# First half's moving operands made in four spaced steps, mean squares later, input rows added ahead of attention, the last pair's combining and loads sooner

## The chip, the cores and the metric

One NeuronCore of one Trainium2 chip. The metric is the device time of one execution in microseconds (us), the median of several runs. PE is TensorE (the matrix engine), DVE VectorE, ACT ScalarE, POOL GpSimd; SP, ACT and POOL also issue DMAs, each in the order of its own queue.

## What is computed

One decoder layer in float32, 2048 tokens by 1024: dilated causal attention (16 heads of 64, dilations 1, 4, 16, mixed by their softmax sums) beside a Mamba-2 scan (16 heads of 64, 2 groups, state 128), each gated and normalised, then one output product and a layer norm.

```python
proj = x @ w_in
q, k, v, z_att, z_ssm, xbc, dt = split(proj)
o1, o2, o3 (with l1, l2, l3) = windowed attention of q, k, v at dilations 1, 4, 16
y_att = rms_norm(softmax_mix(o1, o2, o3) * silu(z_att), att_norm_g)
xs, b, c = split(silu(causal_conv(xbc)))
y_ssm = rms_norm((ssd_scan(xs, dt, a, b, c) + d_skip * xs) * silu(z_ssm), ssm_norm_g)
out = concat(y_att, y_ssm) @ w_out
result = layer_norm(alpha * x + out, ln_g, ln_b)        # alpha = 2 ** 0.25
```

## The kernel before

Every float32 factor is kept as a high part, rounded to the type that PE multiplies quickly, and a low part, the remainder; a product is high x high + high x low + low x high, three matmuls. Making an operand is therefore a copy to `t[:, 0]` on ACT (high) and a subtraction to `t[:, 1]` on DVE (low), then a store to scratch memory in DRAM (names beginning with `d_`).

**0 to 207 us:** the V projection.

**207 to about 1490 us:** 52 jobs, each a 1024-deep product of two column tiles, done with Strassen and Winograd's seven products in place of eight. A product is 12 matmuls of 128 x 128 x 512 into one of five banks `pp` (lines L357, L359, L361). ACT empties a bank with `keep` (L366, tile `ev`), DVE adds (L374). The moving operands have the names B11, T1, B21, T2, B22, T4, T3; T... are differences of quarters. Jobs run in phases: ten on the first half of the tokens, 22 on the second, 12 more, and 8 output jobs (`"o"`) that multiply the scan's branch with W_out and leave their part of the output in `d_o`. After each product `flush()` runs the closures in `later[count]`, the count of products; `after(n, f)` puts `f` n products ahead. This written order is what PE, DVE, ACT and POOL execute; the order on SP's queue is set by a scheduler.

In the first phase four further things are made between the products: the second half's moving operands from x (`sums_part`, tiles `st` to `to`, stored to `d_T`), W_out's moving operands from rows times a gain (`output_side`, tiles `woraw` to `wot`, stored to `d_U`), the scan's gate (`fin_zs`, tile `ez`, to `d_zs`), and the decays of dt (`decays`, on DVE).

The scan has 32 units (16 blocks x 2 groups), one begun every four products from product 161 (about 740 to 1290 us). A unit goes through `ssd1` to `ssd7` in steps of a product; its matmuls use three banks `ss`. `ssd6` squares the gated rows and reduces them (L646, tile `bsh`), `ssd7` sums the result over the partitions with a matmul by ones (L651). `zt` is the gate's load.

**1490 to 2010 us:** attention, eight pairs of heads, 24 steps each, numbered (d, qd, half): `scores` (PE, L896; mask and minimum on DVE, L904; exponential on ACT, L912), `transposes` (L925, L927) and `values` (L945). `load_dil` brings a mask table `tb` and `v`. When a pair is through, `statistics` and `gather` send its sums through DRAM, `weights` makes the mixing weights on DVE, stored and loaded back broadcast as `wb`, and `combine` mixes the three results, for pairs 0 to 6 on POOL in four calls during the next pair (L1016, L1025, L1031), and stores columns of the attention branch, as raw rows in `d_ua` and, for row tiles 0 to 2, split in `d_uh`. Pair 7 is combined on DVE at the end.

**2010 us to the end:** sixteen row tiles of 128 tokens times W_out's attention half (`load_w`, eight tiles of 1 MB). For tiles 0 to 3 `product_early` does seven columns of eight, from `fetch_early`, and `product_last` the one of pair 7 (`e7`); for 4 to 15 `product` does all. Each tile is fetched raw (`fetch_raw`), split (`split`: L1081 high on ACT, L1082 low on DVE), squared (`squares`: L1087, L1088), and after its product `add` scales and adds it to `O[n]`, loaded from `d_o` by `residual_load` (L1093) after `residual_add` (L1099) added the input row there (L1096). `norm` is the layer norm: statistics (L1182, L1184), square root on ACT (L1186), normalising on DVE (L1196), gain and bias on POOL (L1197, L1198), and the store (L1199). `O[n]` of tile n uses the buffer of tile n - 4.

## Time and profile before

| what | value |
|---|---|
| runs | 2268.11, 2277.9 and 2277.93 us, median 2277.9 |
| profiled execution | 2259.55 us, its span 2257.7 us |
| mean granted clock of PE | 0.955 |
| DMA | 551.78 MB, mean 244 GB/s |

The span is the time from the profile's first to its last instruction; the execution's own time is a little longer. "Busy" is the share in which an engine executes. A row of waits reads: engine, what it was about to do and its line, `<-` what it waited for, then total us, times, and the longest. A row of a timeline reads: start, length, engine, line, operation, output `<-` inputs, with the idle time ahead in brackets. The granted clock is 1.00 or 0.50 in each moment.

### The profile page before, as it was taken

How to read it: one execution, taken by the hardware profiler on the slowest of the kernel's cores; microseconds unless marked ns; L12 is line 12 of the kernel's file. 1: busy time of each engine (PE TensorE's matmuls, PEld its weight loads, DVE VectorE, ACT ScalarE, POOL GpSimd, SP SyncE). 2: the span in 40 equal slices, each digit the busy share in tenths (PEclk: the TensorE clock that was granted, in tenths of full speed). 3: DMA queues.
4: the chain of work that ended last, by engine and by line, in shares of the span. 5: the costliest groups of instructions: out<-in, count | busy, mean ns of one | idle time of the engine just before them, and what ended most of it. 6: DMA issues, size and time to landing. Idle time of an engine off the chain costs nothing.

```text
span 2257.7 us, 39253 instructions
## 1 busy us (share of the span) xinstructions
PE 2066.3 (92%) x13768; PEld 1708.4 (76%) x13768; DVE 1438.5 (64%) x3235; ACT 1204.7 (53%) x3128; POOL 1188.7 (53%) x978
## 2 busy tenths in 40 slices
PE   7999896869999999988999989989999999988698
PEld 7998775648887777867777768878878887766576
DVE  3432654538999668755555433338888888856777
ACT  3331444425655676755656534447888888842121
POOL 2113444556887566664445344432566666770544
PEclk9999998989999999999999999979999999999899
DMA  9989675795777877799787893253687777796443
GB/s 334 370 316 332 232 272 204 246 389 162 226 219 267 313 262 274 261 344 342 230 271 248 293 366 111 100 181 131 197 244 215 199 218 227 214 338 190 157 170 111
DMA packets 273046, 551.78 MB, mean 244 GB/s; under 512 B 44689, under 2 KB 129553, under 8 KB 256081
## 3 DMA queue, kind: packets, MB, share of 16 engines
q1 hardware_dynamic: 185696, 261.09, 35.8%
q0 software_dynamic: 36448, 193.34, 24.0%
q10 hardware_dynamic: 50704, 94.84, 13.4%
q8 instruction: 109, 1.79, 0.3%
q14 instruction: 89, 0.72, 0.1%
HBM read 359.39 MB, written 206.57 MB: 251 GB/s over the span
## 4 chain that ended last, share of the span: by engine, by line
PE 34%; DMA 10%; DVE 9%; ACT 8%; issue 4%; POOL 2%; ACTq 1%; SPq 0%; DVEq 0%; POOLq 0%
PE S L896 5%; PE N L945 5%; PE T L925 5%; PE pp L357 5%; PE pp L359 5%; PE pp L361 5%; DMA zt<-d_zs 3%; ACT P L912 2%; ACT mt L578 1%; DVE P L904 1%; DMA TB22l<-d_UT 1%; DMA d_kl<-ev 1%; PE ss L618 1%; DMA kl<-d_kl 1%; DMA w<-d_wc 1%
## 5 line engine op out<-in xcount | busy, mean ns | idle before, releaser
L313 POOL TENSOR_TENSOR w<-wr,w 128x512 fp32r<-128x512 f32 x287 | 437.5, 1540 | 284.6 <-ACT w L312 212.4
L912 ACT ACTIVATE P<-P,st 128x256 f32<-128x256 f32 (+1 forms) x768 | 345.1, 451 | 99.4 <-DVE st L904 98.7
L904 DVE CUSTOM_DVE_ANT_0 P<-S,tb 128x256 f32<-128x256 f32 (+1 forms) x768 | 235.1, 362 | 87.0 <-PE S L896 49.6
L366 ACT COPY ev<-pp 128x512 f32<-128x512 f32 x208 | 121.1, 582 | 288.4 <-PE pp L361 188.7
L374 DVE TENSOR_TENSOR ev<-pp,ev 128x512 f32<-128x512 f32 x184 | 122.1, 684 | 167.4 <-PE pp L361 101.1
L927 DVE COPY PT<-T 128x512 f32<-128x512 f32 (+1 forms) x304 | 196.5, 677 | 1.4 <-PE T L925 1.4
L305 DVE TENSOR_TENSOR wr<-wr 128x512 f32<-128x512 f32 x164 | 173.2, 1056 | 35.7 <-DMA wr<-w 24.7
L312 ACT CAST w<-wr 128x512 fp32r<-128x512 f32 x287 | 171.2, 618 | 38.4 <-DVE wr L305 23.2
L925 PE MATMUL T<-ident,P 128*128 128x128 f32 x1200 | 179.3, 287 | 5.9 <-DVE PT L927 5.5
L945 PE MATMUL N<-PT,v 128*64 128x128 f32 x2400 | 176.8, 284 | 0.0
L945 PEld LDWEIGHTS N<-PT,v 128*64 128x64 f32 x2400 | 129.5, 138 | 33.3 <-issue 22.8
L925 PEld LDWEIGHTS T<-ident,P 128*128 128x128 f32 x1200 | 130.1, 143 | 30.3 <-DVE PT L927 7.2
L1016 POOL TENSOR_TENSOR wb<-num,wb 128x2048 f32<-128x2048 f32 x21 | 96.3, 4587 | 97.0 <-DMA wb<-d_wd 81.3
L912 ACT ACTIVATION_READ_ACCUMULATOR P<-P,st 128x1 f32 x768 | 143.8, 187 | 0.0
L896 PE MATMUL S<-kh,qp 64*128 64x256 f32 (+1 forms) x1024 | 126.5, 306 | 0.0
L414 DVE SCALAR_TENSOR_TENSOR ev<-ev 128x512 f32<-128x512 f32 x64 | 69.1, 1093 | 65.1 <-ACT ev L413 65.1
L463 DVE SCALAR_TENSOR_TENSOR acc<-U,cw,acc 128x2048 f32<-128x2048 f32 x36 | 106.5, 2959 | 3.4 <-ACT acc L460 3.0
L896 PEld LDWEIGHTS S<-kh,qp 64*128 64x128 f32 x1024 | 88.9, 188 | 22.1 <-issue 20.4
L148 PE MATMUL pp<-vh,xh 128*128 128x256 f32 (+1 forms) x320 | 91.4, 292 | 15.1 <-ACT xh L171 15.1
L357 PE MATMUL pp<-TT3h,w 128*128 128x512 f32 x176 | 77.1, 438 | 29.8 <-ACT ev L366 29.6
L141 POOL TENSOR_TENSOR vl<-vraw,vh 128x256 fp32r<-128x256 f32 (+1 forms) x32 | 29.9, 938 | 131.4 <-ACT vh L140 130.1
L357 PE MATMUL pp<-TB22h,w 128*128 128x512 f32 x208 | 87.1, 419 | 10.5 <-ACT ev L366 6.1
(476 smaller groups left out, 6084.5 us busy)
## 6 DMA issues: line engine op xcount, KB each, us to landing
wr<-w ACTq DMA_DIRECT2D x157, 256.0 KB
v<-d_v POOLq DMA_DIRECT2D x24, 1024.0 KB, 7.1
d_wc<-w SPq DMA_DIRECT2D x44, 512.0 KB
w<-d_wc POOLq DMA_DIRECT2D x44, 512.0 KB, 6.5
wb<-d_wd SPq DMA_DIRECT2D x42, 512.0 KB
csb<-d_cs ACTq DMA_DIRECT2D x32, 512.0 KB
st<-xT SPq DMA_DIRECT2D x31, 512.0 KB
d_v<-vt SPq DMA_DIRECT2D x16, 512.0 KB
```

The lines of the kernel that those rows point to most:

```text
L305: tt = lambda o, a, b, op=OP.subtract: nc.vector.tensor_tensor(q[o], q[a], q[b], op=op)
L312: nc.scalar.copy(t[:, 0], q[nm])
L313: nc.gpsimd.tensor_tensor(t[:, 1], q[nm], t[:, 0].bitcast(F32), op=OP.subtract)
L357: nc.tensor.matmul(ps, w[:, 0, k], th[:, k], start=start and k == 0, stop=False, skip_group_check=not start)
L366: nc.scalar.copy(e, ps)
L374: nc.vector.tensor_tensor(e, a, e, op=op)
L896: nc.tensor.matmul(ov(sp[h][:, 256 * b:256 * b + w]), A["q"][d][x][hr, blk], kv(A["k"][y][hr]), start=(m == 0), stop=(m == 2))
L904: nc.vector.tensor_tensor_reduce(P[:, h, b, 256 - w:256], sp[h][:, c0:c0 + w], tab[:, h, tab.shape[2] - w:], 1.0, 3.0e38, OP.add, OP.min, ...
L912: nc.scalar.activation(p, p, AF.Exp, bias=stat(A, 0, d, h, blk), scale=-1.0, accum_out=stat(A, 1, d, h, blk))
L925: nc.tensor.transpose(tp[:, h, b], P[:, h, b, 128 * which:128 * which + 128], ident)
L927: nc.vector.tensor_copy(pt[:, :, bl[0]:2], tp[:, :, bl[0]:2])
L945: nc.tensor.matmul(nm[64 * h:64 * h + 64, bq * 128:bq * 128 + 128], v[:, k, 64 * h:64 * h + 64], pts[which][:, h, b], start=(f or not whic ...
```

## The change

*Spaced steps.* `in_steps` puts one item of the first half in four successive products: subtraction, high, low, store. `token_sums` and `output_side` use it; loads come earlier, W_out's rows on SP's queue in eight buffers rather than ACT's in four, and the separate gain pass is gone (the gain is a factor in the copy and in the remainder). `ez` is one tile per column tile, stored on its own.

*Mean squares.* The reduction is `ssd7`, one product later, and the matmul `ssd8`, two later; `zt` is loaded one earlier.

*Input rows.* `fin_o` adds alpha times the input on DVE before `d_o` is stored; `residual_add` and its loads are gone at the end. The output jobs' first two operands lie in the buffers of attention's keys and queries.

*Attention.* Pair 0's tables are loaded on POOL's queue, its keys and queries within the last job. During pair 7 the weights and combining of pair 6 come earlier, loads of W_out partly too, and `fetch_early` takes all seven columns at once. At the end pair 7's `wb` loads stand ahead of rows, which move to ACT's and POOL's queues; squares are spread; norms 0 to 3 come after product 4; normalising is on ACT.

```diff
+        def in_steps(c, dst, k, name, o, bufs, queue, make=None, gain=None):
...
+            if make:
+                put(c, make)
+            put(c + 1, high)
+            put(c + 2, low)
+            put(c + 3, store)
+        def token_sums(k, b):
...
+                R[nm] = sums.tile([128, 512], F32, name="st", bufs=5)
...
+            for n, x in ((-7, ("11", 0, 0)), (-5, ("12", 0, 1)), (-4, ("22", 1, 1)), (-3, ("21", 1, 0))):
+                put(max(b + n, 0), lambda x=x: load(*x))
...
+                in_steps(b + c, d_T[1, nm], k, "to", lambda o=o: R[o], 3, nc.sync,
+                         lambda o=o, a=a, d=d: nc.vector.tensor_tensor(R[o], R[a], R[d], op=OP.subtract))
-                    R[nm] = sums.tile([128, 512], F32, name="woraw", bufs=4)
-                    nc.scalar.dma_start(R[nm], wout[e * 128:e * 128 + 128, c * 512:c * 512 + 512])
+                    R[nm] = sums.tile([128, 512], F32, name="woraw", bufs=8)
+                    nc.sync.dma_start(R[nm], wout[e * 128:e * 128 + 128, c * 512:c * 512 + 512])
-            def gain():
...
+                in_steps(at(c), d_U[nm], k, "wot", lambda o=o: R[o], 4, nc.gpsimd, make, gain)
-                output_side(k, 35 + 8 * k)
+                token_sums(k, 7 + 7 * k)
+                at = lambda c, k=k: 37 + (7 * k + c) * 30 // 28
+                output_side(k, at, 35 if k < 2 else 37 + (7 * k - 1) * 30 // 28 - 4)
-                if (ci, q) == (1, 0):
-                                          [[512, 128], [128 * 512, 16], [1, 128]]),
+                if q != ci:
+                                          [[512, 128], [128 * 512, 16], [1, 64]]),
-                for d, f in ((0, ssd1), (1, ssd2), (2, ssd3), (3, ssd4), (4, ssd5), (5, ssd6), (6, ssd7)):
-            after(n0 + 7, out_plan)
+                for d, f in ((0, ssd1), (1, ssd2), (1, ssd3), (3, ssd4), (4, ssd5), (5, ssd6), (6, ssd7), (8, ssd8)):
+            after(n0 + 9, out_plan)
                 nc.scalar.activation(e, e, AF.Copy, scale=msq[:, n:n + 1])
+                nc.vector.scalar_tensor_tensor(e, X[n, q], ALPHA, e, op0=OP.mult, op1=OP.add)
                 nc.sync.dma_start(d_o[n][:, 512 * q:512 * q + 512], e)
+                row_load(rows_.index((n, q)) + 2)
-            nc.sync.dma_start(tb, tabs[...])
+            (nc.gpsimd if pr == 0 else nc.sync).dma_start(tb, tabs[...])
-                    if pr and at in ((0, 3, 0), (0, 3, 1)):
+                    if pr and at[:2] == (0, 2 if pr == 7 else 3):
                         weights(pairs[pr - 1], half)
-                    step = ((1, 0, 0), (1, 1, 0), (1, 3, 0), (2, 0, 0) if pr == 7 else (2, 2, 0))
+                    if pr == 7:
+                        step = ((0, 3, 0), (1, 0, 0), (1, 1, 0), (1, 2, 0))
-                        fetch_early(0, 0, 6)
+                        fetch_early(0)
-                    elif at == (2, 3, 0):
-                        for n in range(2):
-                            fetch_early(n, 6, 7)
+            w3 = [weight_load(A, d) for d in range(3)]
+            for n in range(2):
+                fetch_raw(n, nc.scalar)
+            for n in range(4):
+                residual_load(n, nc.scalar)
-                residual_add(n)
-            for n in range(F):
-                norm(n)
+                if n == F:
+                    for i in range(F):
+                        norm(i)
-            nc.vector.tensor_scalar(o, o, mv[:, 0:1], sd_, op0=OP.subtract, op1=OP.mult)
+            nc.vector.tensor_scalar(nm, mv[:, 0:1], sd_, -1.0, op0=OP.mult, op1=OP.mult)
+            nc.scalar.activation(o, o, AF.Identity, bias=nm, scale=sd_)
```

How the order stands at three places. First ACT, in the first half where W_out's first items are made, before and then after (`w` and `wr` are the stationary operand, `ev` the emptied bank):

```order
L366 COPY ev<-pp 128x512
L236 ACTIVATE woraw<-woraw,gc 128x512 x4
L312 CAST w<-wr 128x512 x2
L243 CAST wot<-woraw 128x512
L312 CAST w<-wr 128x512
L366 COPY ev<-pp 128x512
L243 CAST wot<-woraw 128x512
L312 CAST w<-wr 128x512
```

```order
L127 CAST wot<-woraw 128x512
L329 DMA wr<-w 128x512
L404 COPY ev<-pp 128x512
L129 ACTIVATE wot<-woraw,gc 128x512
L350 CAST w<-wr 128x512
L465 ACTIVATE ez<-ev 128x4x16x8
L129 ACTIVATE wot<-woraw,gc 128x512
L350 CAST w<-wr 128x512
```

The gain pass of four is gone, and a copy with a gain is an ACTIVATE that reads `gc`.

Second PE, around one mean square, before and after; `ss<-one,bsh` is the mean square's matmul, `ss<-xdeh` the unit's state product:

```order
L357 MATMUL pp<-TT1h,w 128x512
L359 MATMUL pp<-TT1l,w 128x512
L361 MATMUL pp<-TT1h,w 128x512
L651 MATMUL ss<-one,bsh 128x1
L357 MATMUL pp<-TB21h,w 128x512
L359 MATMUL pp<-TB21l,w 128x512
L361 MATMUL pp<-TB21h,w 128x512
```

```order
L395 MATMUL pp<-TT2h,w 128x512
L397 MATMUL pp<-TT2l,w 128x512
L399 MATMUL pp<-TT2h,w 128x512
L694 MATMUL ss<-one,bsh 128x1
L672 MATMUL ss<-xdeh,bsh 128x512
L672 MATMUL ss<-xdel,bsh 128x512
L672 MATMUL ss<-xdeh,bsl 128x512
L605 MATMUL ss<-ident,xs 128x128 x4
```

The matmul stood after a T1 product, right behind the reduction's product; now it stands 26 rows later, just ahead of the following unit's state product.

Third DVE at the end, from the last additions to the first norm, before and after:

```order
L1099 SCALAR_TENSOR_TENSOR kl<-wb,kl 128x1024
L1170 TENSOR_TENSOR v<-S,v 128x512 x2
L1172 RECIPROCAL st<-st 128x1
L1176 SCALAR_TENSOR_TENSOR kl<-v,st,kl 128x512 x2
L1182 BN_STATS st<-kh 128x6 x2
L1184 BN_AGGR st<-st 128x2
L1187 RECIPROCAL st<-st 128x1
L1196 TENSOR_SCALAR kh<-kh,st 128x1024
```

```order
L1231 SCALAR_TENSOR_TENSOR kl<-v,st,kl 128x512 x2
L1141 COPY P<-PT 128x128
L1143 TENSOR_TENSOR qp<-P,qp 128x1024
L1149 TENSOR_REDUCE tb_21939<-P 128x128
L1237 BN_STATS st<-kh 128x6 x2
L1239 BN_AGGR st<-st 128x2
L1242 RECIPROCAL st<-st 128x1
L1252 TENSOR_SCALAR st<-st 128x1
```

`residual_add` (L1099) is gone, norm 0 stands behind split and squares of tile 5, and its last operation is a scalar one.

More of the change, by code (lines that the diff above doesn't have):

```diff
@@ L660, in rms, with row_load @@
             nc.vector.reciprocal(msq, msq)
+        rows_ = [(2 * i + ci, q) for i in range(8) for ci, q in ((0, 0), (0, 1), (1, 1), (1, 0))]
+        X = {}
+        def row_load(j):
+            if j < len(rows_):
+                n, q = rows_[j]
+                X[n, q] = xp_.tile([128, 512], F32, name="x", bufs=2)
+                nc.scalar.dma_start(X[n, q], xc[n * 128:(n + 1) * 128, 512 * q:512 * q + 512])
         def fin_o(i):
@@ L784, in hybrid_layer @@
                     after(3, ssd_plan)
[L785 to L789 removed]
+                if m + 1 == len(jobs):
+                    pairs[0] = dict(pr=0, num=[], tab={}, v={}, q={0: []}, k=[])
+                    after(1, lambda: load_qk(pairs[0]))
                 U2, Un = Un, None
@@ L1011, in combine @@
             if d < 3:
[L1012 to L1015 removed]
+                wb = wb or weight_load(A, d)
                 eng.tensor_tensor(wb, A["num"][d], wb, op=OP.mult)
```

241 lines of the change are left out of this document (124 added, 117 removed).

## The prediction

> **What bounds the kernel now.** The page first, then busy time by stretch, cut where the kernel's stages end, then what TensorE (PE) waited for. In the second view the columns are the stretch, its length, each engine's busy time with its instructions, the mean granted clock, the share of DMA time and GB/s.
>
> ```profile
> PE 2066.3 (92%) x13768; PEld 1708.4 (76%) x13768; DVE 1438.5 (64%) x3235; ACT 1204.7 (53%) x3128; POOL 1188.7 (53%) x978
> ```
> ```profile
> 207.00:462.00 255.00, 212.09 (x850) 169.65 (x849) 141.25 (x184) 111.41 (x199) 131.30 (x123) 0.90 0.72 243
> 740.00:1290.00 550.00, 514.39 (x2779) 420.70 (x2780) 345.03 (x581) 357.37 (x727) 313.07 (x277) 0.97 0.83 282
> 1290.00:1490.00 200.00, 191.18 (x816) 155.46 (x815) 60.92 (x77) 79.56 (x141) 87.49 (x77) 0.97 0.57 204
> 1496.81:1530.94 34.13, 31.38 (x208) 24.67 (x208) 16.44 (x97) 19.22 (x88) 10.43 (x18) 0.50 0.33 114
> 1530.94:1562.50 31.56, 31.56 (x379) 26.04 (x377) 28.01 (x110) 26.12 (x98) 9.12 (x14) 1.00 0.60 212
> 2010.00:2127.00 117.00, 79.55 (x346) 63.29 (x343) 70.50 (x87) 19.97 (x34) 36.44 (x18) 0.84 0.66 206
> 2127.00:2257.70 130.70, 117.27 (x498) 92.99 (x498) 99.83 (x131) 24.93 (x41) 59.26 (x21) 0.96 0.41 146
> ```
> ```profile
> PE pp L357 <- ACT ev L366: 39.6, 11, 9.7
> PE ss L651 <- DVE bsh L646: 31.3, 17, 3.6
> PE S L1117 <- ACT num L1081: 17.6, 1, 17.6
> PE S L1117 <- DMA num<-d_uh: 13.6, 2, 9.1
> PE S L896 <- DVE st L904: 5.2, 1, 5.2
> ```
>
> PE is the bound, and what can be won is its idle time (2257.7 - 2066.3 = 191 us) and busy time at half clock. Four places hold most of it, and the change touches all four: the first half (207 to 462), the scan units (740 to 1290), the start of attention (one wait, then 34.13 us at clock 0.50), and the end (2010 on).
>
> **First half.** The length of a product comes from two equal points of neighbouring products in an undisturbed stretch.
>
> ```profile
> 601.61 0.39 PE L357 MATMUL pp<-TT4h,w 128*128 128x512 f32 x1
> ...
> 604.33 0.39 PE L357 MATMUL pp<-TT3h,w 128*128 128x512 f32 x1
> ```
>
> That is 2.72 us; ten jobs of seven products need 190 us and took 255. Idle is 255 - 212.1 = 42.9, half clock the other 22 (212.1 - 190). What ACT, whose copies empty the banks, waited for there, and what was stored:
>
> ```profile
> ACT to L112 <- DVE st L110: 37.1, 9, 8.3
> ACT woraw L236 <- DMA woraw<-wout: 28.9, 6, 9.8
> ACT wot L243 <- DVE woraw L241: 22.9, 10, 4.1
> ```
> ```profile
> d_UT<-wot POOLq DMA_DIRECT2D x13, 512.0 KB, 5.4
> d_UB<-wot POOLq DMA_DIRECT2D x12, 512.0 KB, 4.9
> ```
>
> The change takes away all three: the subtraction runs one product ahead of the copy that reads it, the rows of W_out come at least six products (16 us) ahead where the longest wait was 9.8, and the separate gain pass of ACT is folded in. These 89 us of ACT waiting reached PE as 33.8 of the 39.6 us in the first row of waits (the other 5.8 lie outside this stretch). I leave 5 of the 33.8 for the decay chain, also on DVE, that stays. New is waiting for buffers: a `wot` tile comes round after four items (4 x 30/28 products, 11.7 us) of which copy, remainder and store issue take two products (5.4), so 6.3 us are left for a landing of about 5.2 (the two medians). A `to` tile has three buffers, and once in each group of four its reuse comes one product after the store's issue. Bounds on PE are 0 (PE can run about two products ahead) and 33.8 (all comes back); I take 7, nearer the medians. So 34 - 5 - 7 = 22 of idle and, as half the cause of the 22 us at half clock goes, 8 of that: **30** (12 to 40). The 16 loads of W_out move from ACT's queue to SP's, where they stand among stores whose tiles are free for longer than a load's issue takes; four quarter loads of x per group replace two, on SP still; the gate `ez` is written in 256-byte runs by 16 DMAs instead of 8, of the same bytes: 0, hidden while stores land in time.
>
> The Trainium skill, "DMA: Bandwidth & Descriptors", Specifications, speaks against this: below 512 B a write is read, modified and written. By it these 8 MB would cost more DMA time and the sum would be unchanged unless landings lengthen, which is the slower rival below. No row here shows its price.
>
> **Scan units.** The reduction goes one product later, and the matmul that waits on it two (26 rows of PE's order), past the 3.6 us of the longest wait: 31.3 goes. Bounds for the new order: that matmul now stands just ahead of the next unit's state product, so four tiles share three banks in one product. The bank is freed by the state update on DVE, 684 ns each:
>
> ```profile
> L634 DVE TENSOR_TENSOR H<-H,ss 128x512 f32<-128x512 f32 x28 | 19.1, 684 | 25.2 <-PE ss L632 16.3 <-POOL H L614 8.6
> ```
>
> Nothing at one end, its whole 19.1 at the other; I take 6 since most updates end before PE needs the bank. Mean clock 0.97 over 550 us is at most 16 us, of which I take 4. **29** (14 to 38). The gate's load, one product earlier on ACT's queue, and the later creation of its sum's tile are on DVE's path only: 0.
>
> **Input rows.** 32 additions of 128x512 on DVE, at 0.75 us (L1176 below, the same form) 24 us, in a stretch where DVE is busy 61 of 200; 32 loads on ACT's queue where DMA is at 0.57. Both hidden: 0. If that cover were gone, at most 24. The first two output operands now lie in attention's buffers, so the loads of pair 0's keys and queries, on POOL's queue, wait for the last job's second product; the bound is that product, 2.72, and 0 is taken since the tables behind them have ten more.
>
> **Attention starts.** The three tables go from SP's queue, where they stood behind the output's stores, to POOL's, so the 5.2 us wait, which DVE's mask passed on, becomes one for the first `v` load, whose conditions do not change; the loads of keys are written out one job earlier, which they were in effect. I take **2**. The other end is 5 plus the half clock, 31.38/2 = 15.7: 21.
>
> **Last pair and end.** POOL's combining of pair 6, then DVE's way to the 17.6 us wait:
>
> ```profile
> 1979.79 4.57 POOL L1016 TENSOR_TENSOR wb<-num,wb 128x2048 f32<-128x2048 f32 x1 [15.75 <-ACT P L912]
> ...
> 2006.02 1.11 POOL L1054 DMA_DIRECT2D qp<-d_wo  x2
> 2007.11 0.71 POOL L1069 DMA_DIRECT2D num<-d_uh  x1
> 2007.81 0.55 POOL L1054 DMA_DIRECT2D v<-d_wo  x1
> 2008.96 4.52 POOL L1031 TENSOR_TENSOR wb<-wb 128x2048 f32<-128x2048 f32 x1 [0.59 <-DMA wb<-d_za]
> ```
> ```profile
> 2114.00 2.70 DVE L1099 SCALAR_TENSOR_TENSOR kh<-wb,kh 128x1024 f32<-128x1024 f32 x1 [2.88 <-DMA kh<-d_o]
> ...
> 2116.88 1.41 DVE L1176 SCALAR_TENSOR_TENSOR kh<-T,st,kh 128x512 f32<-128x512 f32 x2
> ...
> 2120.28 1.47 DVE L1196 TENSOR_SCALAR kh<-kh,st 128x1024 f32<-128x1024 f32 x1
> 2121.68 2.36 DVE L1080 COPY P<-PT 128x128 f32<-128x128 f32 x1
> 2125.14 2.21 DVE L1082 TENSOR_TENSOR num<-P,num 128x1024 fp32r<-128x1024 f32 x1 [1.11 <-ACT num L1081]
> ```
> ```profile
> L1099 DVE SCALAR_TENSOR_TENSOR kl<-wb,kl 128x1024 f32<-128x1024 f32 x6 | 7.3, 1220 | 0.0
> ```
>
> The combining of pair 6 is six passes of 4.5 to 4.6 us in POOL's order, the last with the gate. Before, the issues of 1.11, 0.71 and 0.55 us stand in that row, and the gate is waited for 0.59: 3.0. Now those issues come behind it, and two of the five earlier loads ahead of its first product. Its start is two attention steps sooner in the order (2 x 520/192 = 5.4 us), but the small transfers of pair 6's statistics have as much less time to arrive. DVE runs the weights between the steps of attention, so if the statistics are late, the mask and the copies of later steps queue behind on DVE and PE waits for them: bounds 0 and 5.4, and I take 1 on PE, and 2 of the 5.4 for POOL. So the result of pair 6 is there 5 us sooner.
>
> The first operand of the end is now fetched whole, where it was fetched first without pair 6's column and then with it. So its fetch has to wait for pair 6's store, which it did not: the first wait (9.1) shrinks by only 3 (bounds: 5 longer, all of it gone). The second (13.6 - 9.1 = 4.5) goes, as there is no second fetch, with 2 or 3 of half clock. Pair 7's weights are loaded ahead of the rows that nobody needs yet, on ACT's queue where rows stood before; so its column should be there when the four early products end. Less the 1 above this makes 9.
>
> The 17.6 stays in kind. Product 6 needs split 6, which stands on DVE behind the addition of row 4; that waits for a buffer whose chain is norm 0, two passes on POOL, its store and the load of row 4. Before, four additions of 1.22 (L1099) stood ahead of norm 0; they are gone (4.9), while a square reduction and a split of about 2 us together move in: 3 sooner. Behind the load, from 2114.00 on, 2.70 (the addition) and 1.47 (the normalisation) fall out, and a scalar operation comes in: 4. That is 7 (bounds 0 and 17.6).
>
> Later tiles lose 1.22 and the normalisation's 1.47 or less of DVE in each round, enough to end the short waits there:
>
> ```profile
> PE S L1119 <- DVE num L1082: 2.7, 4, 1.0
> PE S L1119 <- DVE qp L1082: 1.2, 2, 0.6
> PE T L1119 <- DVE num L1082: 1.1, 2, 0.6
> ```
>
> I take 4 of these 5. The normalisation goes to ACT, busy 25 of 131 us there: hidden. Together 9 + 7 + 4 = **20** (6 to 33). Behind it the last tile's own norm and store set the end as before.
>
> **Sum.** 30 + 29 + 0 + 2 + 20 = 81 off the profiled execution's 2259.55 gives 2178. The runs shown are 8.6 to 18.4 us above that one (median 2277.9, 0.8%), so the time to compare is 2178 x 1.0081 = **2196**.
>
> **Rivals.**
> 1. Store landings hold ACT in the first half: 8 instead of 30, so 2218. For: the medians leave one microsecond of room in the `wot` ring and none in the other, and DMA is at 0.72 there; against: PE can run two products ahead.
> 2. The end wins nothing, as the whole fetch waits for pair 6's store as long as before: 2216.
> 3. The clock stays full at the start of attention: 15.7 less, 2180. For: the same work goes on at full clock from 1530.94 (clock 1.00 in the first view). Against: the wait for `v` is taken to leave some 3 us idle. The Trainium skill, "TensorE: Matmul & The Clock Gate", What's actually happening, has one busy window of about 3.4 us restore it, by which this loss should be about 2 us and not 15.7, and the sum 14 more. The trace disagrees: 34.13 us at 0.50, of which 31.38 are busy.
> 4. Slower: the two rings become the pace. With landing time L a `wot` item needs (5.4 + L)/4 instead of 2.9 us, 28 times, a `to` item (5.4 + L)/3 instead of 4.8, 16 times: a loss of 12.3 L - 91. It outweighs the other 51 from L = 11.5, and with the 18.3 below, seen where operands are reloaded, it is 134: 2259.55 + 83 is 2343, or 2362 as a median. For it: the stage gets shorter and DMA denser (0.72 to 0.82). Against: the same stores landed in about 5.
> ```profile
> d_UT<-wot POOLq DMA_DIRECT2D x4, 512.0 KB, 18.3
> ```
> 5. The bank sharing eats the scan units' gain (19.1 and its clock): 2214.
>
> **Chances.** Forecast 0.50 (2178 to 2214), rival 1 0.18, 2 0.10, 3 0.10, 5 0.07, slower 0.05. The range goes from the forecast's good end with rival 3 (2178 - 16, so 2160) to rivals 1 and 2 together with some margin (2238, so 2243). Within 0.5% (11 us) is about what a measurement here cannot tell from no change; only rivals 1, 2 and 5 together or a milder form of 4 come there, 0.04. Slower is 0.05, faster 0.91.
>
> **What would show it.** Right: between 207 and 462 no ACT wait on `woraw`, PE idle below 22; no waits of the mean-square matmul on DVE; one wait instead of two before the first early product; 8 to 12 us before product 6 in place of 17.6; no short waits after it. Wrong: ACT waiting on stores of `wot` or `to` for over 20 us, PE waiting on `ss` banks, or the combining of pair 6 ending after 2012.

## The result, and the profile after

In runs taken side by side the changed kernel took 2250.19 us (2242.01 to 2251.73), the kernel before 2273.01 (2263.86 to 2277.93): a ratio of 0.9897 [0.9852, 0.9942]. That is 23 us shorter, where 82 were forecast, and outside the range. The profiled execution after is the longest of its runs, the one before is shorter than all the runs beside it, so the two spans, 2257.7 and 2250.0 us, differ by only 7.7. The stage table is for where the time went, not for how much it was in all.

The table is worked out from the start times of PE's own rows in the two traces, and in that of the last experiment, which has the change with four of its parts altered.

| stretch, us | before | after | last experiment |
|---|---|---|---|
| start to the first job's third product | 219.4 | 218.5 | 217.8 |
| from there to the 12th job's third product | 296.5 | 279.8 | 268.1 |
| the next ten jobs | 193.6 | 205.0 | 202.6 |
| from there to the first unit of the scan | 44.2 | 40.1 | 39.7 |
| scan units, first to last | 507.6 | 508.1 | 485.6 |
| from there to attention's first score | 230.7 | 229.9 | 229.6 |
| first score to the end of pair 0 | 76.1 | 83.4 | 74.0 |
| pairs 1 to 7 | 436.3 | 444.6 | 451.4 |
| last score to the end | 253.3 | 240.6 | 246.0 |
| span | 2257.7 | 2250.0 | 2214.8 |

Busy time by engine from the page, and by stretch, for the changed kernel. The columns are those of the prediction's view; the stretches are the same places of the program, moved with it.

```profile
PE 2059.8 (92%) x13768; PEld 1707.0 (76%) x13768; DVE 1487.2 (66%) x3252; ACT 1216.9 (54%) x3131; POOL 1184.1 (53%) x980
```
```profile
206.00:446.00 240.00, 205.91 (x851) 166.33 (x850) 160.46 (x187) 105.60 (x186) 135.91 (x124) 0.92 0.79 262
730.00:1280.00 550.00, 511.52 (x2778) 419.44 (x2779) 362.54 (x583) 357.43 (x727) 316.06 (x277) 0.98 0.83 282
1280.00:1480.00 200.00, 191.39 (x823) 156.20 (x822) 94.86 (x107) 82.08 (x141) 91.08 (x78) 0.98 0.67 236
1485.19:1526.15 40.96, 31.46 (x214) 25.25 (x216) 21.55 (x89) 18.02 (x83) 12.66 (x20) 0.50 0.42 133
```

In the first row PE idles 240 - 205.9 = 34.1 us, where the forecast was under 22. In the second it idles 38.5, where before it was 35.6: nothing was won. The stretch at half clock is 40.96 us, where it was 34.13. What PE waited for in the whole span of the changed kernel, then ACT's waits in the first half:

```profile
PE pp L395 <- ACT ev L404: 42.6, 12, 9.1
PE S L1172 <- DMA num<-d_uh: 16.7, 1, 16.7
...
PE S L1172 <- ACT num L1142: 11.3, 1, 11.3
PE S L953 <- DMA kl<-d_kl: 9.9, 4, 7.6
PE ss L609 <- DVE msq L699: 8.8, 5, 2.0
PE ss L609 <- DVE msq L697: 7.7, 5, 2.2
PE S L953 <- DVE st L961: 5.4, 1, 5.4
```
```profile
ACT ez L465 <- DMA d_zs<-ez: 25.9, 4, 12.4
...
ACT wot L127 <- DMA d_UB<-wot: 14.6, 5, 8.7
ACT wot L129 <- DMA d_UT<-wot: 10.9, 7, 4.0
...
ACT wot L127 <- DMA d_UT<-wot: 7.4, 2, 7.1
```

L395 starts a product and L404 empties its bank, so the first row is the 39.6 us row of before, still there. What changed is what keeps ACT from the bank: no longer mainly `st` and `woraw` but, first, `ez`, the gate's tile, and then `wot`. `ez` is now one buffer per column tile: the next column tile can't be written until the store of the last one has landed. The stores of `wot` also land later than before (the DMA issues of this stretch: KB each, and median us from issue to landing; it was 5.4 and 4.9):

```profile
d_UT<-wot POOLq DMA_DIRECT2D x14, 512.0 KB, 7.3
d_UB<-wot POOLq DMA_DIRECT2D x12, 512.0 KB, 7.3
```

L609 is the first matmul into the second of the two banks with which a scan unit opens. It waits for L697 and L699, DVE's reading of an older unit's mean square out of one of the three banks. These ten waits, 16.5 us, stand where the 17 of 31.3 us were, and small waits on other operands make up the rest. At attention's start L953, a scores matmul, waits for the last part of pair 0's keys (7.6) and for DVE's mask L961 (5.4). DVE's own waits there (1475 on) have a row that was not there before, the addition of an input row in the last output job:

```profile
DVE ev L719 <- DMA x<-xc: 7.0, 2, 5.8
```

In the last pair the mixing weights of pair 6 are stored by SP and loaded back. SP's rows before, and then after (`d_uh<-uh` is an earlier store on the same queue, 192 KB each):

```profile
1959.54 3.15 SPq L1039 DMA_DIRECT2D d_uh<-uh  x2
1970.91 0.36 SPq L1001 DMA_DIRECT2D d_wd<-cm  x1
1972.60 3.69 SPq L1014 DMA_DIRECT2D wb<-d_wd  x6
```
```profile
1963.41 3.17 SPq L1101 DMA_DIRECT2D d_uh<-uh  x2
1969.34 0.36 SPq L1058 DMA_DIRECT2D d_wd<-cm  x1
1977.03 3.04 SPq L1064 DMA_DIRECT2D wb<-d_wd  x5
```

The same 48 KB store (`d_wd<-cm`) lets its loads go after 1.7 us before and after 7.7 us now. POOL's rows after show what is new ahead of it, two loads of 1 MB, and what waits behind:

```profile
1965.95 0.59 POOL L1116 DMA_DIRECT2D kh<-d_wo  x1
1966.53 0.55 POOL L1116 DMA_DIRECT2D kl<-d_wo  x1
1984.39 4.57 POOL L1078 TENSOR_TENSOR wb<-num,wb 128x2048 f32<-128x2048 f32 x1 [17.31 <-DMA wb<-d_wd]
...
2011.18 4.56 POOL L1093 TENSOR_TENSOR wb<-wb 128x2048 f32<-128x2048 f32 x1
```

What the two queues sent between the issue of the store and 1974.5 (packets, MB, share of DMA time; q0 is POOL's, q1 is SP's) shows where the store stood:

```profile
q0 software_dynamic: 247, 1.89, 93.0%
q1 hardware_dynamic: 247, 0.13, 12.1%
```

SP's 247 packets are of 512 B, and they belong to the second `d_uh` store ahead on the same queue; the 128 B packets of the 48 KB come only after them. The queues take turns, packet for packet, but POOL's packets are of 8 KB. So the loads held up the store ahead, and that one the small store.

The combining of pair 6 starts at 1984.39, where it was 1979.79, although the store was issued 1.6 us sooner. All of attention lies 5.0 us later in this profile (last score at 2009.4, before at 2004.4). Counted from the last score, the store goes 6.6 us sooner than before, and the combining starts 0.4 and ends 2.7 us sooner.

### The profile page after: what moved, and what is told of

Its sections match the earlier page's. It is cut to its first block, busy times and chain, and to the rows that moved or that the text cites. A ratio compares the mean times of both kernels' runs of the same rounds, so it can differ in the third digit from the quotient of the medians.

```text
span 2250.0 us, 39433 instructions
## 1 busy us (share of the span) xinstructions
PE 2059.8 (92%) x13768; PEld 1707.0 (76%) x13768; DVE 1487.2 (66%) x3252; ACT 1216.9 (54%) x3131; POOL 1184.1 (53%) x980
## 5 line engine op out<-in xcount | busy, mean ns | idle before, releaser
L351 POOL TENSOR_TENSOR w<-wr,w 128x512 fp32r<-128x512 f32 x287 | 432.2, 1520 | 291.5 <-ACT w L350 199.1
L961 DVE CUSTOM_DVE_ANT_0 P<-S,tb 128x256 f32<-128x256 f32 (+1 forms) x768 | 235.3, 362 | 87.7 <-PE S L953 50.9
L404 ACT COPY ev<-pp 128x512 f32<-128x512 f32 x208 | 120.9, 581 | 254.8 <-PE pp L399 163.6
L350 ACT CAST w<-wr 128x512 fp32r<-128x512 f32 x287 | 171.1, 618 | 54.2 <-DVE wr L343 34.7
L343 DVE TENSOR_TENSOR wr<-wr 128x512 f32<-128x512 f32 x164 | 181.6, 1107 | 24.5 <-DMA wr<-w 12.6
L953 PE MATMUL S<-kh,qp 64*128 64x256 f32 (+1 forms) x1024 | 126.1, 306 | 0.0
L395 PE MATMUL pp<-TB22h,w 128*128 128x512 f32 x208 | 89.5, 430 | 36.5 <-ACT ev L404 34.4
L503 DVE SCALAR_TENSOR_TENSOR acc<-U,cw,acc 128x2048 f32<-128x2048 f32 x36 | 114.0, 3167 | 6.2 <-ACT acc L500 5.8
L953 PEld LDWEIGHTS S<-kh,qp 64*128 64x128 f32 x1024 | 88.8, 188 | 22.0 <-issue 20.5
L397 PE MATMUL pp<-TB22l,w 128*128 128x512 f32 x208 | 87.8, 422 | 5.2 <-DMA TB22l<-d_T0B 2.1
```

Of the source, the lines that this page charges most:

```text
L343: tt = lambda o, a, b, op=OP.subtract: nc.vector.tensor_tensor(q[o], q[a], q[b], op=op)
L350: nc.scalar.copy(t[:, 0], q[nm])
L351: nc.gpsimd.tensor_tensor(t[:, 1], q[nm], t[:, 0].bitcast(F32), op=OP.subtract)
L404: nc.scalar.copy(e, ps)
L503: return lambda: nc.vector.scalar_tensor_tensor(acc[0], U[:, j:j + 16, :], cw[:, i, j:j + 1], acc[0], op0=OP.mult, op1=OP.add)
L953: nc.tensor.matmul(ov(sp[h][:, 256 * b:256 * b + w]), A["q"][d][x][hr, blk], kv(A["k"][y][hr]), start=(m == 0), stop=(m == 2))
```

## Experiments

In all of them the stages are those of the table. Stages that an edit does not touch vary too: the ten jobs after the first half took 196.2 to 205.0 us in the eight profiles in which nothing of the first half was altered. A few us in one stage of one profile are thus no finding by themselves.

**The first half: which buffer holds ACT?** Room for a second `ez` buffer had to come from two other pools, so a control has only that: four `st` buffers for five, six `woraw` for eight, with their loads later.

```diff
-  R[nm] = sums.tile([128, 512], F32, name="st", bufs=5)
+  R[nm] = sums.tile([128, 512], F32, name="st", bufs=4)
...
-  R[nm] = sums.tile([128, 512], F32, name="woraw", bufs=8)
+  R[nm] = sums.tile([128, 512], F32, name="woraw", bufs=6)
...
```

> The changed kernel with only the room made that the next two need: the tiles st have four buffers instead of five and woraw six instead of eight, and their loads come correspondingly later. A control. Theory (the gate's single buffer is what ACT waits for): within 5 us of the changed kernel's 2250, the 45 us of ACT waiting for stores of ez still there. Rival (the loads of rows are what matters): ACT waits on loads of st or woraw by over 10 us more, and the first half gets 5 to 15 us longer.

Measured 2253.05 us, 0.9934 [0.9907, 0.9961]; the first half's row of the table is 280.2 (after 279.8). The room costs nothing there. Then the control with two buffers:

```diff
-  t[ci] = cp.tile([128, 16, 8, 8], F32, name="ez", bufs=1)
+  t[ci] = cp.tile([128, 16, 8, 8], F32, name="ez", bufs=2)
```

> As the control, with two buffers for the gate's tile ez; its 16 stores in runs of 256 bytes stay. Theory A (the single buffer: the second tile's SiLU waits for the store of the first to land, 7 to 12 us each, and PE for ACT): ACT's waits on ez fall from 45 us to under 8, PE's waits on ACT's copies between 207 and 530 from 31 us to under 16, and the span gets 15 to 25 us shorter than the control's. Rival B (the short runs keep DMA busy, so other stores land later and other rings take over): ACT's waits move to wot, and the span gains less than 8.

Measured 2244.06 us, 0.9882 [0.9847, 0.9916]; first half 272.5. And the control with the gate's tile as it was before the change, both column tiles in one, stored at once:

```diff
-  t[ci] = cp.tile([128, 16, 8, 8], F32, name="ez", bufs=1)
+  t = cp.tile([128, 16, 2, 8, 8], F32, name="ez", bufs=1)
...
-  if q != ci:
...
-  [[512, 128], [128 * 512, 16], [1, 64]]),
...
+  if (ci, q) == (1, 0):
...
+  [[512, 128], [128 * 512, 16], [1, 128]]),
```

> As the control, with the gate's tile and store as in the kernel before: one tile for both column tiles, one store in runs of 512 bytes. Theory A (only the wait matters): the same as with two buffers, within 4 us. Rival B (the short runs matter too): shorter than with two buffers by 8 us or more, and stores of wot land sooner.

Measured 2242.79 us, 0.9889 [0.9856, 0.9923]; first half 267.5. PE's wait for ACT's copies from 207 to 530, in the control, with two buffers, and with the old tile:

```profile
PE pp L395 <- ACT ev L404: 36.6, 7, 9.4
```
```profile
PE pp L395 <- ACT ev L404: 20.8, 7, 4.8
```
```profile
PE pp L395 <- ACT ev L404: 20.0, 6, 6.3
```

The single buffer costs 16 of the 36 us of waiting, and with it 8 to 13 us of the stage, about half of the 15 to 25 that were expected. What stays comes with ACT's waits on `wot`, which hardly shrank (47.6 us in the control, 44.9 with two buffers, 43.4 with the old tile). With the old tile this stretch is 29.0 us shorter than in the kernel before (267.5 against 296.5): close to the 30 of the forecast. The totals of the last two are 9 and 10 us below the control's; as the intervals of the ratios overlap a little, that size is not settled, but the waits show the place.

**The mean squares.** The matmul stands 8 products behind the start of its unit (+8). Two runs put it at +7 and at +10:

```diff
-  ... (6, ssd7), (8, ssd8)):
+  ... (6, ssd7), (7, ssd8)):
```

> The changed kernel with the mean square's matmul one product earlier (7 instead of 8 products after the unit's start; the reduction stays at 6). Theory C (its bank: at 8 it is the first of four tiles in one product, three banks, so a transpose of the next unit but one waits until DVE has read the mean square): PE's 16.5 us of waits on msq vanish, the old wait on the reduction stays away (under 5 us), and 740 to 1280 gets 15 to 22 us shorter. Rival D (DVE is simply late in this stage): the 16.5 us go and come back as waits on the reduction or other DVE results; under 6 us.

Measured 2287.22 us, 1.0082 [1.0054, 1.0110], slower than the kernel before; scan units 539.1. PE's largest wait in the scan units:

```profile
PE ss L694 <- DVE bsh L689: 43.4, 24, 4.5
```

At +7 no unit opens in the same product and the bank waits are gone; but the matmul is again too soon for DVE's reduction and waits longer than before the change, as the reduction itself has moved one product back. So the change needs both: room behind the reduction, and a product in which nothing else wants a bank.

```diff
-  ... (6, ssd7), (8, ssd8)):
+  ... (6, ssd7), (10, ssd8)):
...
-  after(n0 + 9, out_plan)
+  after(n0 + 11, out_plan)
```

> The changed kernel with the mean square's matmul at 10 instead of 8 products after the unit's start, when no other of the three banks is asked for. Theory D, restated after the run at 7 (DVE is 4 us or more behind PE here, so whatever PE asks of it within two products shows as a wait; at 8 it was the bank): with two products of room on either side both waits go, 740 to 1280 gets 15 to 22 us shorter than in the changed kernel. Rival I (DVE or ACT is the pace of this stage, the waits move to the next thing that PE needs of them): under 6 us.

Measured 2229.33 us (2228.0 to 2233.0, no run as long as the shortest after), 0.9827 [0.9796, 0.9858]; scan units 485.3 in place of 508.1. The largest waits there are now

```profile
PE ss L605 <- DMA xs<-d_xs: 3.4, 1, 3.4
PE ss L605 <- DVE y L652: 3.3, 2, 1.7
PE ss L609 <- DVE H L674: 2.8, 1, 2.8
```

and no mean square is among them. A unit opens every four products, so at +8 the matmul meets the opening of the unit two behind it, `ssd1`, and its bank is wanted in that very product; at +10 only the next unit's reduction is there. Of the edits to this change this is the largest: 22.8 us of the stage, 21 between the medians.

**Attention's start.** First the input rows' loads on SP's queue, on the theory that ACT's casts, and behind them POOL's loads of keys, are held up by these loads on ACT's queue:

```diff
-  nc.scalar.dma_start(X[n, q], xc[n * 128:(n + 1) * 128, 512 * q:512 * q + 512])
+  nc.sync.dma_start(X[n, q], xc[n * 128:(n + 1) * 128, 512 * q:512 * q + 512])
```

> The changed kernel with the input rows of the output jobs loaded on SP's queue and not on ACT's. Theory G (on ACT's queue each load waits for DVE's addition to free its buffer, ACT's casts of the last job's weights stand behind that, and the first loads of attention behind those on POOL, 5 us later than before relative to the last job): the loads of keys and queries are issued about 5 us sooner, the 7.6 us wait for them goes, the start of attention gets 5 to 8 us shorter. Rival H (the loads themselves land later, 15 against 13 us, from other traffic): 0 to 2 us.

Measured 2241.17 us, 0.9884 [0.9849, 0.9919]; first score to the end of pair 0 is 85.7, not shorter than 83.4. Its waits of PE and of DVE there:

```profile
PE S L953 <- DVE st L961: 8.2, 1, 8.2
PE S L953 <- DMA kl<-d_kl: 5.9, 1, 5.9
```
```profile
DVE ev L719 <- DMA x<-xc: 5.9, 2, 5.1
```

The keys' wait falls (7.6 to 5.9) and the mask's grows (5.4 to 8.2), since the last input row still lands late. So it is the row, not its queue. Next, the rows of the last two row tiles added at the end:

```diff
-            if j < len(rows_):
+            if j < len(rows_) - 4:
...
-                nc.vector.scalar_tensor_tensor(e, X[n, q], ALPHA, e, op0=OP.mult, op1=OP.add)
+                if n < 14:
+                    nc.vector.scalar_tensor_tensor(e, X[n, q], ALPHA, e, op0=OP.mult, op1=OP.add)
...
+                if n > 13:
+                    nc.vector.scalar_tensor_tensor(O[n], X[n], ALPHA, O[n], op0=OP.mult, op1=OP.add)
```

> The changed kernel with one part altered: the input rows of the last two row tiles (14 and 15) are not added ahead of attention; they are loaded and added at the end, where all were before the change. Theory: the last job's input row, which lands late behind attention's first loads, holds the vector engine (7.0 us on x, 2 waits, in the changed kernel), and with it the mask statistics on which attention's second score waits 5.4 us; without it both go, the four casts of the scalar engine are less held back, and first score to the first pair's end takes 76 to 79 us in place of 83.4; the time is 4 to 7 us shorter if nothing at the end asks for the two rows back (two vector instructions of some 1.3 us each are added there). Rival: the second score then waits as long for something else that lands late behind the same loads (83 us stays, the time as the changed kernel's within 2 us).

Measured 2238.09 us, 0.9874 [0.9851, 0.9897]; 73.4 in place of 83.4, shorter than before the change (76.1). All that PE still waits for there is

```profile
PE S L954 <- DMA kl<-d_kl: 3.8, 1, 3.8
```

The mask's wait is gone whole, and last score to the end is no longer (237.9, after 240.6). The stage gained 10 us, more than expected; in the total the intervals overlap the changed kernel's, so the 12 us between the medians are not secured by themselves.

**The last pair and the end.** The old places of pair 6's combining, of the W_out loads and of the split fetch:

```diff
-  if pr and at[:2] == (0, 2 if pr == 7 else 3):
+  if pr and at[:2] == (0, 3):
...
-  step = ((0, 3, 0), (1, 0, 0), (1, 1, 0), (1, 2, 0))
+  step = ((1, 0, 0), (1, 1, 0), (1, 3, 0), (2, 0, 0))
...
-  fetch_early(0)
+  fetch_early(0, 0, 6)
...
```

> The changed kernel with the last pair's part of attention as in the kernel before: pair 6's weights and combining at their old steps, W_out's tiles loaded at the old steps, the first two operands fetched in six columns and then one. Theory E (in the changed kernel two 1 MB loads of W_out, issued ahead of the small stores that pair 6's weights go through, keep those stores from landing for 7.7 us where it was 1.7, so the combining ends later, 2017 against 2015, though it was asked for sooner, and the whole fetch waits for it): the wait before the first early product falls from 16.7 to about 9 and one of about 4 comes back; together 3 to 6 us shorter from the end of attention's scores to the end. Rival F (the store of pair 6 is late because of the other loads at the end, whatever the steps): no change within 2 us in that stretch.

Measured 2245.27 us, 0.9896 [0.9856, 0.9937]: the same. The first product of the end starts 15.6 us after the last score in place of 24.7, and from there to the end it takes 224.6 in place of 215.9: 240.2 in place of 240.6.

```profile
PE S L1173 <- ACT num L1143: 12.8, 1, 12.8
PE N L1179 <- DVE tb L1150: 7.2, 2, 6.2
PE S L1173 <- DMA num<-d_uh: 6.5, 2, 4.6
```

The 48 KB store lets its loads go after 4.1 us here. The wait of 16.7 has become two of 6.5 together, and in their place PE waits 7.2 for DVE (2.7 in the changed kernel) and 12.8 before product 6 (11.3). My reading: what follows the early products needs pair 7, whose own chain through DRAM (sums stored, gathered, weights stored, loaded back) is as late either way; the loads of its weights were issued 34.7 us after the last score in the changed kernel and 33.0 here. So that chain was tried next: this edit (the old places) again, and the large loads of pair 7 held on POOL's queue until its small transfers have passed. Only the second part is shown:

```diff
...
-            fetch_early(2)
-            fetch_raw(3, nc.gpsimd)
...
-            gate(1, nc.vector)
-            gate(2, nc.vector)
+            gate(1, nc.gpsimd)
+            gate(2, nc.gpsimd)
+            fetch_early(1, 0, 7)
+            fetch_early(2, 0, 7)
+            fetch_raw(3, nc.gpsimd)
+            nc.gpsimd.dma_start(w7, d_wo[7].rearrange("p a c -> p (a c)"))
```

> The changed kernel with the last pair's combining and loads put back to their old places, and the large loads of pair 7 (early operands of row tiles 1 and 2, raw rows of tile 3, one tile of the output weights) held on the POOL queue until pair 7's own small transfers have passed. Theory: the chain behind pair 7 (statistics stored, gathered, weights, weights stored, loaded to all partitions, combining), which ends some 66 us after the last score in the kernel before and after alike, is stretched by small stores that land 6 to 11 us late behind 1 MB loads; with these loads behind it, it ends some 55 us after the last score, first score to first product is 16 us in place of 24.7, and the time 8 to 12 us shorter. Rival: the early products then wait for the operands that are fetched later, and what the chain wins is given back there: first product to the end grows by as much or more (time as the changed kernel's or longer).

Measured 2261.19 us, 0.9954 [0.9934, 0.9973]: 11 us above the changed kernel, the intervals overlapping a little. ACT's rows for the chain in the changed kernel, and in this experiment:

```profile
2017.93 3.35 ACTq L1034 DMA_DIRECT2D d_st<-sT  x4
2028.94 0.39 ACTq L1040 DMA_DIRECT2D cm<-d_st  x1
...
2037.72 0.38 ACTq L1058 DMA_DIRECT2D d_wd<-cm  x1
2044.07 3.73 ACTq L1064 DMA_DIRECT2D wb<-d_wd  x6
```
```profile
2022.74 1.84 ACTq L1034 DMA_DIRECT2D d_st<-sT  x4
2029.57 0.39 ACTq L1040 DMA_DIRECT2D cm<-d_st  x1
...
2044.51 0.38 ACTq L1058 DMA_DIRECT2D d_wd<-cm  x1
2053.88 4.51 ACTq L1064 DMA_DIRECT2D wb<-d_wd  x6
```

The theory fell. The stores land sooner (6.8 us from the first issue to the gather, 11.0 in the changed kernel), but the gather with the making of the weights and the store of the weights are slower (14.9 and 9.4 us against 8.8 and 6.4), and PE, after a first wait of 5.5, waits another 8.5 us for operands that are fetched later. The loads of the weights are issued 39.7 us after the last score, 6.7 later than with the old places alone (33.0), and the end comes 7.1 later after it (247.3 against 240.2). The other profiles agree with the reading above: in all thirteen that have the change or an edit of it, the first of these loads is issued 31.9 to 41.8 us after the last score, and the span ends 205.7 to 207.7 us after that issue. In the kernel before, the two are 39.3 and 214.1. So the end moves with this point nearly one for one, whatever the waits of PE between. No run moved this point alone.

Last, the splits two tiles ahead in place of one:

```diff
-                if n < 15:
-                    split(n + 1)
-                    squares(n + 1)
+                    split(n + 2)
+                    squares(n + 2)
...
```

> The changed kernel with the split and squares of the row tiles two tiles ahead of their product instead of one, so that tile 6 is split before row 4 is waited for. Theory J (the 11.3 us before product 6 are the split queued on DVE behind the addition that waits for row 4): that wait falls under 3 us and the rest of the end takes no new wait of over 5: 8 to 13 us shorter, with the half clock around it. Rival K (the addition of row 4 itself holds the banks, so the wait moves to product 7): under 5 us.

Measured 2253.25 us, 0.9914 [0.9878, 0.9949]. Its waits from 1960 on:

```profile
PE S L1172 <- DMA num<-d_uh: 17.6, 1, 17.6
PE T L1172 <- ACT num L1142: 5.2, 1, 5.2
PE N L1178 <- DVE tb L1149: 2.0, 1, 2.0
PE N L1178 <- ACT st L1221: 1.7, 1, 1.7
```

The 11.3 falls to 5.2 and 1.7, yet first product to the end is 214.2 in place of 215.9. Removing 4.4 us of this wait is worth 1.7 us, less than can be told apart.

**Together.** The old `ez` with its room, +10, the last rows at the end, the splits two ahead, and the held-back loads with the old places that belong to them:

```diff
-  t[ci] = cp.tile([128, 16, 8, 8], F32, name="ez", bufs=1)
+  t = cp.tile([128, 16, 2, 8, 8], F32, name="ez", bufs=1)
...
-  ... (6, ssd7), (8, ssd8)):
+  ... (6, ssd7), (10, ssd8)):
...
-            if j < len(rows_):
+            if j < len(rows_) - 4:
...
+            gate(1, nc.gpsimd)
+            gate(2, nc.gpsimd)
...
+                    split(n + 2)
...
```

> Together: the first half's early products of the weights stored as in the kernel before (their own tile form, no single buffer waited for), with two tile pools made smaller and their loads later to make room; the mean-square product at ten positions behind its scan unit in place of eight; the last two row tiles' input rows added at the end; pair 7's small transfers ahead of its large loads; the splits two tiles ahead at the end. Theory: the losses are separate and add: 13 us in the first half up to the operand reload (of the changed kernel's 279.8), 22 us in the scan stage (508.1 to 485.3), 0 to 5 at attention's start, 0 to 10 in the last pair and the end: 2200 to 2215 us, about 0.972 to 0.977 of the kernel before. Rival: what the first half wins is lost in the attention stages, which start earlier but wait for the same transfers and end at the same clock, and the time stays at that of the mean-square edit alone (2229, 0.9827).

Measured 2219.05 us, 0.9780 [0.9763, 0.9798]: between the two theories, nearer the first. Up to the last score it is 35 us ahead of the changed kernel (1974.2 against 2009.4), and then takes 248.1 in place of 240.6. So the held-back loads were left out, and with them the old places; against the run just shown:

```diff
-            gate(1, nc.gpsimd)
-            gate(2, nc.gpsimd)
+            gate(1, nc.vector)
+            gate(2, nc.vector)
...
```

> The combination once more without the edit that puts pair 7's small transfers ahead of its large loads (last pair and loads stay as in the changed kernel): the first half's weight products stored as in the kernel before, the mean-square product at ten positions, the last two row tiles' input rows at the end, the splits two tiles ahead. Theory: the held-back loads cost the combination some 8 us of its end (last score to the end 248.1 us, where the changed kernel has 240.6 and the splits alone 239.8); without them it ends 238 to 241 us after the last score, at some 2210 to 2214 us, ratio about 0.975. Rival: the long end belongs to the other store form of the first half, with which an earlier experiment also had 247.8 us there, and the time stays at 2219, ratio 0.978.

Measured 2213.20 us (2209.46 to 2216.61), 0.9748 [0.9723, 0.9773], 55 us below the kernel before and the fastest of all. The time is the one expected, but not the way: last score to the end is 246.0 in the profiled execution, the longest of its runs, so the held-back loads do not explain the long end. The three profiles with the old `ez` have 246.0 to 248.1 there, as the rival had it; pair 7's weights are also loaded later in them (40.0 to 41.8 us after the last score, 34.7 in the changed kernel). How a tile of the first half should do that is open. The separate gains add nearly fully up to attention. In pairs 1 to 7, which the altered parts don't touch, the profile has 451.4 us, the changed kernel 444.6, the kernel before 436.3; in all thirteen profiles with the change it is 442 to 451. So the change itself loses there, and the 451.4 is within the spread. PE's largest wait from 1440 to 1970 in this run:

```profile
PE S L952 <- DMA kl<-d_kl: 10.1, 5, 3.0
```

Of these 10.1 us, 2.2 are pair 0's; before, pairs 1 to 7 had 0.5 in all. Such a wait can cost more than itself: in the changed kernel pair 3 waits 1.5 us for its keys, then runs 6.8 us at half clock without an idle moment, and takes 67.4 us in place of 62.5. In the kernel before the last part of a pair's keys was issued 45 to 46 us into the pair ahead and landed 14 to 18 us later, for a pair of 62.5: there was hardly any room. What makes the keys later now was not tried.

## Why the prediction was wrong, step by step

In the two profiles the first half won 16.7 us where 30 were forecast, and the ten jobs behind it lost 11.4; the scan units lost 0.5 (29 were to be won), attention's start 7.3 (2 to be won), pairs 1 to 7 8.3 (no term); the end won 12.7 of 20. The three other rows won 5.8 together.

**First half, 30:** the mechanism was right, one edit was priced wrong. ACT's waits on `st` and `woraw`, 89 us, of which nothing was to stay, fell to 9.3 and 5.7. The step that failed is the last clause on `ez`, "0, hidden while stores land in time". They don't: ACT waited up to 12.4 us for one. The single buffer was to be seen in the diff, and the view of landings was there for `wot` only, whose stores then took 7.3 instead of about 5. The mark set for that, over 20 us of ACT waiting on `wot` or `to`, was passed (32.9 on `wot`). With the old tile 29.0 us were won here: PE idled 21.5 less and was busy 7.5 less (forecast 22 and 8). Part of that came from other waits, for PE's wait on ACT's copies was still 20.0, where the forecast left 12: the 5 and 7 were too little. Two buffers of 256-byte runs took 272.5, the old tile with its longer runs 267.5. The Trainium skill, "DMA: Bandwidth & Descriptors", Specifications, has writes below 512 B read and modified first, which agrees with that sign; but the stores of `wot` landed as late with either (medians 6.5 and 9.4 us against 6.6 and 9.2, from 207 to 530), and one pair of profiles doesn't decide it. Of the 16.7 us that the changed kernel won, 11.4 went in the next ten jobs. The eight profiles of that code, 196.2 to 205.0 against 193.6, make a loss of 3 to 11 likely; as the two runs with another `ez` have it too (197.7 and 200.7), its cause is open.

**Scan units, 29:** the failing step is "Nothing at one end, its whole 19.1 at the other; I take 6 since most updates end before PE needs the bank". The bank sharing was seen, but the reader was the wrong one: not the state update but DVE's reading of the mean square itself. With small waits for other operands the whole gain went, more than rival 5 had it. The gain is real where no bank is wanted: 22.3 us at +10 against before. The trace could not show this wait, but the written order could: +8 is a multiple of the four products between units.

**Input rows, 0:** "Both hidden: 0" failed at the last job. DVE had time for the additions; what it did not have in time is the last row, and attention's first mask stands behind that addition in DVE's order. The other end of the bounds, 24, was for the wrong thing (DVE's time). It cost 10 us at attention's start, and the forecast 2 for that start became 7.3 lost. The keys, for which 0 was taken and 2.72 was the bound, are late too: 3.8 us remain without the rows (0.5 before), and why is open.

**Pairs 1 to 7, no term:** the forecast left this stretch out without a reason, and 8.3 us were lost there. Pair 3, above, has 4.9 of them, and pair 7, where the steps were moved, 2.1, with a wait of 3.1 for `v`.

**Last pair and end, 20:** 12.7 came. Two steps failed. "So the result of pair 6 is there 5 us sooner": against the last score it was 2.7 sooner, as a store of 48 KB landed 6 us later behind a larger one that two loads of 1 MB slowed; the risk had been named ("the small transfers of pair 6's statistics have as much less time") and priced 1 and 2. The combining ended at 2015.7 (the row of 2011.18 above), past the mark of 2012, but 5.0 of that is attention's own delay. And "the first wait (9.1) shrinks by only 3 (bounds: 5 longer, all of it gone)": it is 16.7, outside the bounds, as the whole fetch waits for pair 6's store; before, it was two waits of 13.6. Product 6's 7 was right: 17.6 to 11.3. The short waits of the splits behind it fell from 5.0 to 1.3, as forecast. But the two experiments on these waits, which took 10.2 us off one and 4.4 off the other without moving the end by more than 2, show that both sums were made as if the waits were in series with the end. In the thirteen profiles above the end follows the moment when pair 7's weights are loaded: that came 4.6 us sooner than before, and 8.2 were won behind it.

**The clock, rival 3:** at attention's start the half clock outlasts the waits, as the forecast had it (40.96 us at 0.50, of which 31.46 busy). With the last rows at the end, the stretch that begins when the keys have come shows PE busy all through:

```profile
1478.91:1509.63 30.72, 30.72 (x215) 24.59 (x214) 14.86 (x88) 18.03 (x83) 11.96 (x19) 0.50 0.44 125
```

That is 30.72 us at 0.50 without a single idle us. By the Trainium skill, "TensorE: Matmul & The Clock Gate", What's actually happening, one busy window of 3.4 us would end it; the trace disagrees, here more plainly than before.

## What to carry to other kernels

Price a buffer that becomes single by the landing time of the store that frees it, not by the transfer's size; where no row shows that landing, its lower bound isn't zero. When an instruction moves in a pipelined order, count its new place modulo the pipeline's period and look who else wants its bank in that step. And removing a wait near the end is worth only what the next chain, followed to its own end, leaves of it.

## What was not expected of the hardware

A 48 KB store that landed in 1.7 us by itself took 7.7 us when a 192 KB store stood 3 us ahead of it on its own queue and two loads of 1 MB ran on another. The Trainium skill, "DMA: Bandwidth & Descriptors", Queues, rings and completion order, has each DMA engine take turns between queues packet by packet. The trace agrees: 247 packets of each queue in 5.2 us. But a turn is a packet and not a share of the bytes, so the queue with 512 B packets moved 0.13 MB while the one with 8 KB packets moved 1.89. So this store was late because its own queue had small packets left while the other had large ones; that is read from one trace, and no run varied the packets. And PE stayed at half clock for 30.72 us of uninterrupted work at attention's start, while the same work ran at 1.00 after it.
